# Taking GpSimd's remaining arithmetic out of a five-stage fp32 kernel and giving it to VectorE

## The chip, the cores and the metric

The program runs on one NeuronCore of a Trainium2 chip. A core has five engines that run their own instruction streams: TensorE (PE in the profile; PEld is its weight load), VectorE (DVE), ScalarE (ACT), GpSimd (POOL) and SyncE (SP), and 16 DMA engines. The metric is the device time of one execution in microseconds; lower is better.

## The reference

Everything is float32 on 1024 tokens of width 1024. The first block is an FFN, a token mixer and a second FFN, each with a norm ahead and a norm behind; the second block prepends 16 tokens and applies an even layer (a linear recurrence, RG-LRU, beside a chunked state-space scan, SSD) and an odd layer (stick-breaking attention).

```python
def swiglu(x, w_gate, w_up, w_down):
    return (jax.nn.silu(x @ w_gate) * (x @ w_up)) @ w_down

def partial_rope(t, pos):          # the first 16 of 64 dimensions of a head
    ...
    out = jnp.concatenate([x1 * cos - x2 * sin, x2 * cos + x1 * sin, rest], axis=-1)

def first_block(x, ...):
    f1 = swiglu(rms_norm(x, ffn1_pre_g[l]), ffn1_w_gate[l], ffn1_w_up[l], ffn1_w_down[l])
    x = x + FFN_RESIDUAL_WEIGHT * rms_norm(f1, ffn1_post_g[l])
    m = token_mixer(rms_norm(x, mix_pre_g[l]), w_in[l], ...)
    x = x + rms_norm(m, mix_post_g[l])
    f2 = swiglu(rms_norm(x, ffn2_pre_g[l]), ...)
    x = x + FFN_RESIDUAL_WEIGHT * rms_norm(f2, ffn2_post_g[l])

# SSD of the even layer, in chunks
y_diag = jnp.einsum('bcgls,bgecls,bcsgep->bclgep', cb, decay, X)
y_off = jnp.einsum('bclgn,bcgepn,bgecl->bclgep', Cc, states, jnp.exp(a_cum))
y = (y_diag + y_off).reshape(bsz, L + pad, SSD_HEADS, SSD_HEAD_DIM)
y = y + xh * ssd_d[:, None]
```

## The kernel before

The stages follow one another: first FFN (0 to about 692 us), mixer (from about 705), second FFN (about 1350 to 2035), even layer (about 2050 to 2850), odd layer (to the end). A float32 product is made of three TensorE products: an operand is split into a high part (ScalarE, a rounded copy) and a low part (VectorE, the difference). So a split is one ScalarE and one VectorE instruction, and TensorE waits for the second.

**The order of instructions.** Each piece of work is a Python generator that yields the engine it wants ("P" TensorE, "A" ScalarE, "V" VectorE, "G" GpSimd, "D" DMA) and a planned cost. A planner (`Sched`) picks among the ready requests by priority and planned time, and so writes one fixed order for each engine. On the chip each engine runs its order strictly, and a late instruction holds all behind it. The planner's costs of a VectorE and a GpSimd instruction don't depend on each other.

**FFN.** Both big products use seven block products in place of eight. The differences of token blocks that these need are made in `tokens` (`diff`, lines 796 to 818): the high parts are subtracted on VectorE (L802), the low parts on GpSimd (L804), the two are added (L806), T2 adds two more, and the result is split again (ScalarE, then L815 on VectorE). Tiles named `T` are these. The splits of gate and up weights are L473 (`wl`), those of the down operands L1049 (`dl`), the sums of down's results into `acc` L1104 (`pdn` is PSUM, `sg` SBUF). GpSimd makes the inner sums of h (L956) and of the down weights (L1006), which both versions keep.

Down's last pass (`ci` = 2) finishes rows of 128 tokens one after the other, and `post` (from L1185) then normalises each: sum of squares (ScalarE), the reciprocal root (tiny VectorE instructions L306 to L310), gain and residual. Six of eight rows have the gain multiplied by GpSimd in `scale` (L1220) and then one fused VectorE instruction (L1209); the other two have two VectorE instructions (L1212, L1215). Behind a row come the norm of the next stage (L603), the transposes by TensorE (L554) and the split of the transposed activations (L542), for which the next stage's first product waits.

**Mixer.** A rotary head is copied to `rx`, shuffled into `ry` (L1821), multiplied on VectorE (L1823) and GpSimd (L1825), added on VectorE (L1827), and split; the low half of queries (L1406) and keys (L1427) is GpSimd's.

**Even layer.** Per chunk GpSimd scales X by the decay (L2720). `ssd_back` makes `x*d + psy` in four VectorE instructions (L2780, `psy` is PSUM), then `ea*pso` (L2784), and four GpSimd instructions add `ea` (L2789). `gated` (L2972) multiplies on GpSimd.

Of the kernel before, what the change touches and what calls it, by code (L numbers as in the profile page):

```python
# [18 lines left out]
P = 128  # L19
# [637 lines left out]
def ffn_stage(c, A, first, rows0, wg, wu, wd, gpost, res, rows, nxt, meta=None, cols=None):  # L657
# [12 lines left out]
    with ExitStack() as ctx:  # L670
# [120 lines left out]
        def tokens():  # L791
# [4 lines left out]
            def diff(hi, lo, a, b_, extra, ev):  # L796
# [6 lines left out]
                yield ("G", pool_tt(512))  # L803
                nc.gpsimd.tensor_sub(u, a[1].bitcast(F32), b_[1].bitcast(F32))  # L804
# [284 lines left out]
        def evac_d(ci, p, t, ps):  # L1089
# [95 lines left out]
        def post(t, done):  # L1185
# [4 lines left out]
            scaled = Ev()  # L1190
            on_pool = t not in (5, 7)
            if on_pool:
                sch.spawn(scale(t, scaled), 1, tt)
# [11 lines left out]
            if on_pool:  # L1205
                yield scaled
                yield ev_x[t]
                yield ("V", dve(1024))
                nc.vector.scalar_tensor_tensor(acc[t], acc[t], r, xs[t], op0=ALU.mult, op1=ALU.add)  # L1209
            else:  # L1210
                yield ("V", dve(1024))
                nc.vector.scalar_tensor_tensor(acc[t], acc[t], r, gp[0], op0=ALU.mult, op1=ALU.mult)  # L1212
                yield ev_x[t]
                yield ("V", dve(1024))
                nc.vector.tensor_add(acc[t], acc[t], xs[t])  # L1215
            yield from rows.put(t, acc[t], junk)

        def scale(t, ev):
            t_ = yield ("G", pool_tt(1024))
            nc.gpsimd.tensor_mul(acc[t], acc[t], gp[0])  # L1220
            ev.set(t_)
# [76 lines left out]
        ahead = Stream(c, "G", shared=True)  # L1298
# [36 lines left out]
class Attention:  # L1335
# [58 lines left out]
    def evac_q(self, u, h, src, scale, ps):  # L1394
# [3 lines left out]
        for e in range(2):  # L1398
# [4 lines left out]
            on_pool = ps is None  # L1403
            t = yield ("G", pool_tt(512)) if on_pool else ("V", dve(512))
            if scale == 1.0:
                (nc.gpsimd if on_pool else nc.vector).tensor_sub(q[R2[e], 2 + e], s, hi)  # L1406
# [9 lines left out]
    def evac_k(self, u, tok, src, ps, ev):  # L1416
# [4 lines left out]
        for e in range(2):  # L1421
# [3 lines left out]
            on_pool = ps is None  # L1425
            t = yield ("G", pool_tt(n)) if on_pool else ("V", dve(n))
            (nc.gpsimd if on_pool else nc.vector).tensor_sub(ks[e][o, tok], s, ks[e][R2[e], tok].bitcast(F32))  # L1427
# [197 lines left out]
    def out_proj(self, oD, w_out, after, ready, evac, last=KD - 1):  # L1625
# [10 lines left out]
        def load():  # L1636
            yield after
            WO.extend(c.new_A())
            yield from W.into(w_out, 0, WO[0], WO[1], ev_w, 2, "V" if self.col0 else "GV")
# [77 lines left out]
def mixer_stage(c, A, rows0, prm, w_in, forget_b, lams, subln, rope, w_out, gpost, res, rows):  # L1717
# [3 lines left out]
    with ExitStack() as ctx:  # L1721
# [89 lines left out]
        def rope_evac(u, w, h, ps):  # L1811
# [265 lines left out]
        def out_rows(t, ps, tag):  # L2077
# [24 lines left out]
            eng = "GV"[t // 4]  # L2102
            yield (eng, pool_tt(1024) if eng == "G" else dve(1024))
            (nc.gpsimd if eng == "G" else nc.vector).tensor_add(y, y, x)
            T.r_x.release(sch.free[eng])
# [337 lines left out]
def even_stage(c, A, rows0, prm, w_in, lru_wa, lru_wx, dt_bias, a_log, ssd_d, w_out, meta, res, rows):  # L2443
# [212 lines left out]
    def ssd_front(g):  # L2656
# [7 lines left out]
        for i, (t0, T) in enumerate(CHUNKS):  # L2664
# [54 lines left out]
            yield ("G", pool_tt(512))  # L2719
            nc.gpsimd.tensor_tensor(xe[:T], xd[:T], dec[:T].unsqueeze(2).to_broadcast([T, 8, 64]), op=ALU.mult)  # L2720
# [12 lines left out]
    def ssd_back(g):  # L2733

        St = None
        for i, (t0, T) in enumerate(CHUNKS):
# [44 lines left out]
            ss.release(t)  # L2781
            if i > 0:
                t = yield ("V", dve(512))
# [462 lines left out]
```

## Time and profile before

| what | value |
| --- | --- |
| three runs | 3673.99, 3675.97 (median), 3686.52 us |
| the profiled execution, its own time | 3678.58 us |
| its span (first to last instruction) | 3676.9 us |
| TensorE busy in the span | 94% |
| VectorE, ScalarE, GpSimd busy | 75%, 46%, 17% |
| mean granted TensorE clock | 0.978 of full |

The busy shares are means over stages of different kinds. The sums of the prediction are made against 3678.58 us, the profiled execution's own time, which lies 2.61 us above the median.

### The profile page before, as it was taken

The numbers are of one execution on the slowest core, as the hardware profiler recorded it, in microseconds if no ns is written. First come the engines' busy times: TensorE is split into PE (matmuls) and PEld (weight loads), VectorE is DVE, ScalarE is ACT, GpSimd is POOL, SyncE is SP. The second block draws the span as 40 slices with busy tenths as digits, with TensorE's granted clock in tenths as the row PEclk, the third lists the DMA queues.
The fourth block names the chain that finished last, engine by engine and source line by source line (L and its number), as shares of the span: only waits on it lengthen the run. The fifth ranks groups of instructions, "written<-read, shape, count | busy, mean of one in ns | idle before, by whom it ended". The sixth has DMA issues, their size and how long they took to land. (4 is left out here: it accounts for less than half of the span.)

```text
span 3676.9 us, 51971 instructions
## 1 busy us (share of the span) xinstructions
PE 3469.4 (94%) x19675; PEld 2950.4 (80%) x19675; DVE 2756.6 (75%) x4900; ACT 1694.3 (46%) x3449; POOL 641.5 (17%) x577
## 2 busy tenths in 40 slices
PE   8899999799999899999999899998999999999989
PEld 7688888578878777888887899988878888888867
DVE  7876699977888769766799768568623788878784
ACT  4333244455656643333344437446412565656561
POOL 3211145411110114211354112113100000000000
PEclk9999999899999999999999999999999999999999
DMA  4232372311210342332561334234332111110123
GB/s 147 87 108 100 120 264 69 128 53 43 68 51 28 104 154 82 106 109 89 183 215 52 111 70 79 68 84 87 119 116 92 55 35 30 30 35 26 35 82 104
DMA packets 296627, 332.52 MB, mean 90 GB/s; under 512 B 17620, under 2 KB 220544, under 8 KB 296376
## 3 DMA queue, kind: packets, MB, share of 16 engines
q1 hardware_dynamic: 290584, 308.15, 27.6%
q10 hardware_dynamic: 5792, 21.04, 1.5%
q8 instruction: 155, 2.54, 0.3%
q14 instruction: 96, 0.79, 0.1%
HBM read 250.80 MB, written 78.35 MB: 90 GB/s over the span
## 5 line engine op out<-in xcount | busy, mean ns | idle before, releaser
L336 PE MATMUL pe<-Ah,wh 128*128 128x260 f32 (+1 forms) x1184 | 344.1, 291 | 21.6 <-ACT sz L224 7.5
L338 PE MATMUL pe<-Ah,wl 128*128 128x260 f32 (+1 forms) x1184 | 339.3, 287 | 0.0
L337 PE MATMUL pe<-Al,wh 128*128 128x260 f32 (+1 forms) x1184 | 339.0, 287 | 0.0
L224 ACT CAST wh<-w 128x512 fp32r<-128x512 f32 x280 | 162.5, 619 | 271.1 <-PE pst L337 193.0
L892 DVE TENSOR_TENSOR sg<-sg,pst 128x512 f32<-128x512 f32 x280 | 186.5, 682 | 114.6 <-PE pst L338 114.3
L337 PE MATMUL pst<-Al,wh 128*128 128x512 f32 x640 | 253.4, 396 | 2.2 <-DVE Al L815 2.2
L473 DVE TENSOR_TENSOR wl<-w,wh 128x512 fp32r<-128x512 f32 x280 | 209.9, 772 | 58.9 <-ACT wh L224 57.5
L336 PE MATMUL pst<-Ah,wh 128*128 128x512 f32 x640 | 251.8, 393 | 0.0
L338 PE MATMUL pst<-Ah,wl 128*128 128x512 f32 x640 | 251.6, 393 | 0.0
L337 PE MATMUL pdn<-dl,dh 128*128 128x512 f32 x592 | 233.4, 394 | 16.3 <-DVE dl L1049 16.3
L336 PEld LDWEIGHTS pe<-Ah,wh 128*128 128x128 f32 (+1 forms) x1184 | 225.8, 191 | 26.0 <-ACT sz L224 8.0
L1511 DVE TENSOR_TENSOR tl<-ptr,th 128x512 fp32r<-128x512 f32 (+2 forms) x344 | 198.0, 592 | 63.6 <-ACT th L224 61.2
L224 ACT CAST th<-ptr 128x512 fp32r<-128x512 f32 (+2 forms) x344 | 170.7, 515 | 133.4 <-PE ptr L1560 128.2
L338 PE MATMUL pdn<-dh,dl 128*128 128x512 f32 x592 | 231.7, 391 | 0.0
L336 PE MATMUL pdn<-dh 128*128 128x512 f32 x592 | 231.6, 391 | 0.0
L956 POOL TENSOR_TENSOR h<-h 128x512 f32<-128x512 f32 x88 | 134.5, 1529 | 535.6 <-DVE h L938 530.5
L337 PEld LDWEIGHTS pe<-Al,wh 128*128 128x128 f32 (+1 forms) x1184 | 225.7, 191 | 1.5 <-issue 0.5
L338 PEld LDWEIGHTS pe<-Ah,wl 128*128 128x128 f32 (+1 forms) x1184 | 225.5, 191 | 0.8
L2219 DVE TENSOR_TENSOR_SCAN kt<-kt,onec 128x392 f32<-128x392 f32 (+6 forms) x224 | 202.5, 914 | 26.1 <-ACT kt L224 25.0
L224 ACT CAST wh<-wr 128x1024 fp32r<-128x1024 f32 (+2 forms) x116 | 119.0, 1026 | 212.0 <-PE pwo L3045 121.7
L473 DVE TENSOR_TENSOR wl<-wr,wh 128x1024 fp32r<-128x1024 f32 (+1 forms) x110 | 138.8, 1263 | 86.0 <-ACT wh L224 85.7
L336 PE MATMUL pst<-T,wh 128*128 128x512 f32 x480 | 188.4, 395 | 10.9 <-ACT T L224 10.8
(555 smaller groups left out, 10496.0 us busy)
## 6 DMA issues: line engine op xcount, KB each, us to landing
hD<-h SPq DMA_DIRECT2D x22, 1792.0 KB
w<-in_ffn_w_gate_dram SPq DMA_DIRECT2D x20, 1024.0 KB
w<-in_ffn_w_up_dram SPq DMA_DIRECT2D x20, 1024.0 KB
d<-hD SPq DMA_DIRECT2D x18, 1024.0 KB
wr<-in_even_w_in_dram SPq DMA_DIRECT2D x36, 512.0 KB
wr<-in_odd_w_in_dram SPq DMA_DIRECT2D x32, 512.0 KB
wr<-in_w_in_dram SPq DMA_DIRECT2D x24, 512.0 KB
d<-in_ffn_w_down_dram SPq DMA_DIRECT2D x8, 1024.0 KB
```

What stands on the lines that cost most here:

```text
L224: self.last = _o(*a, **k)
L336: nc.tensor.matmul(ps, wh, xh, start=start, stop=False)
L337: nc.tensor.matmul(ps, wh, xl, start=False, stop=False)
L338: nc.tensor.matmul(ps, wl, xh, start=False, stop=stop)
L473: (nc.gpsimd if eng == "G" else nc.vector).tensor_sub(lo, raw, hi.bitcast(F32))
L892: nc.vector.tensor_add(dst, src, ps)
L956: nc.gpsimd.tensor_sub(q[:, o], q[:, a], q[:, b_])
L1511: nc.vector.tensor_sub(tl[:rows, :n], ptr[:rows, :n], th[:rows, :n].bitcast(F32))
L2219: nc.vector.tensor_tensor_scan(rev, rev, c.one.to_broadcast([P, m]), kt[:, k0 + m:k0 + m + 1], op0=ALU.mult, op1=ALU.mult)
```

## The change

All but the inner sums (L956, L1006), the adds into `acc` of the first two passes of down (L1104, `ci` = 1) and memsets leaves GpSimd for VectorE: the low differences of `tokens` (L804, 32 instructions), 16 adds into `acc` in down's last pass, the gain of `post` (12; all rows now take the two-instruction form, at L1202 and L1205 of the changed kernel), the splits of the next stage's first weights and of some output weights (L473, 12), the rope products (16) and low halves (32), four residual adds behind the mixer, the decay product (18) and the gates (16). In `ssd_back`, `psy` is added into `ea` in one VectorE instruction and the four fused instructions then read `ea`, so that GpSimd's 64 adds are gone with 16 VectorE instructions in their place. TensorE's instructions are the same in number.

```diff
@@ diff(): T1 to T4
-                yield ("G", pool_tt(512))
-                nc.gpsimd.tensor_sub(u, a[1].bitcast(F32), b_[1].bitcast(F32))
+                yield ("V", dve(512))
+                nc.vector.tensor_sub(u, a[1].bitcast(F32), b_[1].bitcast(F32))
...
@@ sums into acc
+                eng = "V" if ci == 2 else "G"
...
-                    yield from add(c01, c01, "G", v)
+                    yield from add(c01, c01, eng, v)
...
-                    eng = "V" if ci == 2 else "G"
                     yield from add(c10, c10, eng, v)
-                    tt = yield from add(c11, c11, "G", v)
+                    tt = yield from add(c11, c11, eng, v)
...
@@ post()
-            on_pool = t not in (5, 7)
-            if on_pool:
-                sch.spawn(scale(t, scaled), 1, tt)
...
-            if on_pool:
-                yield scaled
-                yield ev_x[t]
-                yield ("V", dve(1024))
-                nc.vector.scalar_tensor_tensor(acc[t], acc[t], r, xs[t], op0=ALU.mult, op1=ALU.add)
-            else:
...
+            yield ("V", dve(1024))
+            nc.vector.scalar_tensor_tensor(acc[t], acc[t], r, gp[0], op0=ALU.mult, op1=ALU.mult)
+            yield ev_x[t]
+            yield ("V", dve(1024))
+            nc.vector.tensor_add(acc[t], acc[t], xs[t])
...
-        def scale(t, ev):
-            t_ = yield ("G", pool_tt(1024))
-            nc.gpsimd.tensor_mul(acc[t], acc[t], gp[0])
...
-        ahead = Stream(c, "G", shared=True)
+        ahead = Stream(c, "V", shared=True)
...
@@ rope_evac(); evac_q, evac_k, the decay product and gated change engine in the same way
-            t = yield ("G", pool_tt(512))
-            nc.gpsimd.tensor_mul(y, y, rp[:, 1])
             yield ("V", dve(512))
+            nc.vector.tensor_mul(y, y, rp[:, 1])
+            t = yield ("V", dve(512))
             nc.vector.tensor_add(x, x, y)
...
@@ ssd_back()
+            y = psy
+            if i > 0:
+                t = yield ("V", dve(512))
+                nc.vector.tensor_mul(ea, ea, pso[:, :, :T])
+                ss.release(t)
+                t = yield ("V", dve(512))
+                nc.vector.tensor_add(ea, ea, psy)
+                ss.release(t)
+                y = ea
...
-                nc.vector.scalar_tensor_tensor(x, x, dcol[:, u:u + 1], psy[:, q, :T], op0=ALU.mult, op1=ALU.add)
...
-                t = yield ("G", 4 * pool_tt(P))
-                for q in range(4):
-                    x = XC[4 * g + q][1][:, tk]
-                    nc.gpsimd.tensor_add(x, x, ea[:, q])
-                r_ea.release(t)
+                nc.vector.scalar_tensor_tensor(x, x, dcol[:, u:u + 1], y[:, q, :T], op0=ALU.mult, op1=ALU.add)
+            (r_ea if i > 0 else ss).release(t)
```

The planner decides again with every engine that is changed, so the order moves too. First place: VectorE in the first FFN while T4 is being made. Before:

```order
L806 TENSOR_TENSOR sg<-sg 128x512
L761 TENSOR_TENSOR w<-w 128x4x128
L802 TENSOR_TENSOR sg<-Ah,T_509 128x512
L815 TENSOR_TENSOR T_650<-sg,T_647 128x512
L761 TENSOR_TENSOR w<-w 128x4x128
L806 TENSOR_TENSOR sg<-sg 128x512
L802 TENSOR_TENSOR sg<-Ah,T_509 128x512
L473 TENSOR_TENSOR wl<-w,wh 128x512
L815 TENSOR_TENSOR T_925<-sg,T_924 128x512
L473 TENSOR_TENSOR wl<-w,wh 128x512
L892 TENSOR_TENSOR sg<-sg,pst 128x512 x2
```

In the changed kernel, where the same differences are made:

```order
L806 TENSOR_TENSOR sg<-sg 128x512
L802 TENSOR_TENSOR sg<-Ah,T_509 128x512
L804 TENSOR_TENSOR sg<-Al,T_510 128x512
L815 TENSOR_TENSOR T_648<-sg,T_644 128x512
L806 TENSOR_TENSOR sg<-sg 128x512
L802 TENSOR_TENSOR sg<-Ah,T_509 128x512
L804 TENSOR_TENSOR sg<-Al,T_510 128x512
L815 TENSOR_TENSOR T_801<-sg,T_800 128x512
L806 TENSOR_TENSOR sg<-sg 128x512
```

The low difference L804 now stands on VectorE beside its high one, and the weight splits (L473) and preparations (L761) that stood between the steps have gone to other places in the order. Second place: VectorE at the end of the first FFN's down product, where the first rows are normalised (`rs_` are the reciprocal roots). Before:

```order
L306 TENSOR_SCALAR rs_v<-ssp 128x2
L1049 TENSOR_TENSOR sg<-d,sg 128x512
L1049 TENSOR_TENSOR dl<-d,dh 128x512
L306 TENSOR_SCALAR rs_v<-ssp 128x2
L308 SCALAR_TENSOR_TENSOR rs_a<-rs_y 128x2
L309 TENSOR_TENSOR rs_a<-rs_a,rs_v 128x2
L310 SCALAR_TENSOR_TENSOR rs_y<-rs_a,rs_y 128x2
L1209 SCALAR_TENSOR_TENSOR acc<-acc,rs_y,gp 128x1024
L1049 TENSOR_TENSOR dl<-d,dh 128x512
L308 SCALAR_TENSOR_TENSOR rs_a<-rs_y 128x2
L1209 SCALAR_TENSOR_TENSOR acc<-acc,rs_y,gp 128x1024
```

In the changed kernel, the end of the same piece:

```order
L310 SCALAR_TENSOR_TENSOR rs_y<-rs_a,rs_y 128x2
L308 SCALAR_TENSOR_TENSOR rs_a<-rs_y 128x2
L1104 TENSOR_TENSOR acc<-acc,pdn 128x512
L309 TENSOR_TENSOR rs_a<-rs_a,rs_v 128x2
L1202 SCALAR_TENSOR_TENSOR acc<-acc,rs_y,gp 128x1024
L310 SCALAR_TENSOR_TENSOR rs_y<-rs_a,rs_y 128x2
L1202 SCALAR_TENSOR_TENSOR acc<-acc,rs_y,gp 128x1024
L1205 TENSOR_TENSOR acc<-acc,gp 128x1024 x2
L1202 SCALAR_TENSOR_TENSOR acc<-acc,rs_y,gp 128x1024 x2
L1205 TENSOR_TENSOR acc<-acc,d 128x1024 x2
```

Each row that had one fused instruction (L1209) now has two (L1202, L1205); the tiny L306 to L310 stay where the chain needs them.

## Rows read from the trace of the kernel before

**Rows 1.** The page, busy time of each engine over the span.

```profile
PE 3469.4 (94%) x19675; PEld 2950.4 (80%) x19675; DVE 2756.6 (75%) x4900; ACT 1694.3 (46%) x3449; POOL 641.5 (17%) x577
```

**Rows 2.** Groups of POOL by form: busy us, mean ns, then the idle time ahead.

```profile
L2789 POOL TENSOR_TENSOR xc<-xc,ea 128x128 f32<-128x128 f32 x64 | 42.7, 698 | 120.7 <-DVE ea L2784 120.7
L804 POOL TENSOR_TENSOR sg<-Al 128x512 f32<-128x512 f32 x16 | 37.9, 2384 | 133.3 <-DVE Al L542 109.2 <-DVE sg L806 18.5 <-DVE h L938 5.5
L804 POOL TENSOR_TENSOR sg<-T,Al 128x512 f32<-128x512 f32 x8 | 12.6, 1589 | 26.8 <-DVE sg L806 13.3 <-DVE T L815 8.5 <-DVE h L938 5.1
L1220 POOL TENSOR_TENSOR acc<-acc,gp 128x1024 f32<-128x1024 f32 x12 | 31.1, 2611 | 21.8 <-ACT junk L224 21.8
```

**Rows 3.** The same view for DVE.

```profile
L1049 DVE TENSOR_TENSOR dl<-d,dh 128x512 fp32r<-128x512 f32 x170 | 172.0, 1022 | 4.7 <-ACT dh L224 4.1
L1104 DVE TENSOR_TENSOR acc<-acc,pdn 128x512 f32<-128x512 f32 x152 | 95.5, 676 | 0.1
L1209 DVE SCALAR_TENSOR_TENSOR acc<-acc,rs_y,d 128x1024 f32<-128x1024 f32 x8 | 10.1, 1279 | 0.1
```

**Rows 4.** Timeline of DVE and POOL: start us, us, operation.

```profile
486.67 2.73 POOL L1006 TENSOR_TENSOR d<-d 128x1024 f32<-128x1024 f32 x1 [1.90 <-DVE dl L1049]
487.06 2.47 DVE L1104 TENSOR_TENSOR acc<-acc,pdn 128x512 f32<-128x512 f32 x4
699.59 2.39 POOL L1220 TENSOR_TENSOR acc<-acc,gp 128x1024 f32<-128x1024 f32 x1 [3.30 <-ACT junk L224]
699.67 2.32 DVE L308 SCALAR_TENSOR_TENSOR rs_a<-rs_y 128x2 f32<-128x2 f32 x1
```

**Rows 5.** Busy us by stage: PE, PEld, DVE, ACT, POOL, then PE clock.

```profile
40.00:140.00 100.00, 87.55 (x379) 68.98 (x379) 88.89 (x127) 33.71 (x60) 43.68 (x23) 0.97 0.12 40
460.00:644.00 184.00, 183.26 (x807) 151.02 (x806) 173.41 (x210) 87.37 (x155) 92.54 (x44) 1.00 0.47 166
660.00:680.00 20.00, 13.59 (x51) 10.39 (x51) 19.82 (x21) 8.26 (x18) 13.55 (x5) 0.85 0.42 133
680.00:705.00 25.00, 19.40 (x83) 15.70 (x81) 24.90 (x42) 14.43 (x30) 7.43 (x4) 0.78 0.43 148
1380.00:1480.00 100.00, 92.46 (x389) 72.55 (x390) 92.00 (x133) 36.88 (x64) 40.87 (x22) 0.97 0.22 71
2200.00:2600.00 400.00, 372.14 (x3012) 356.09 (x3012) 297.72 (x513) 225.16 (x367) 87.22 (x106) 0.96 0.38 80
```

**Rows 6.** Timeline, the differences T1 to T4: idle before, releaser in brackets.

```profile
81.60 1.76 DVE L806 TENSOR_TENSOR sg<-sg 128x512 f32<-128x512 f32 x1 [5.19 <-POOL sg L804]
106.70 0.80 PE L336 MATMUL pst<-T,wh 128*128 128x512 f32 x1 [5.09 <-ACT T L224]
```

**Rows 7.** Timeline, end of the first FFN and start of the mixer.

```profile
664.60 10.79 POOL L1220 TENSOR_TENSOR acc<-acc,gp 128x1024 f32<-128x1024 f32 x4 [5.42 <-ACT junk L224]
665.66 4.70 DVE L1049 TENSOR_TENSOR dl<-d,dh 128x512 fp32r<-128x512 f32 x2
675.99 0.79 PE L337 MATMUL pdn<-dl,dh 128*128 128x512 f32 x1 [5.37 <-DVE dl L1049]
705.08 0.50 PE L336 MATMUL pd<-Ah,wh 128*128 128x512 f32 x1 [0.35 <-DVE Al L542]
```

**Rows 8.** Timeline, the same place in the second FFN.

```profile
2019.18 0.80 PE L337 MATMUL pdn<-dl,dh 128*128 128x512 f32 x1 [5.36 <-DVE dl L1049]
```

**Rows 9.** Timeline, first rotary head of the mixer.

```profile
726.09 2.53 POOL L1825 TENSOR_TENSOR ry<-ry,rope 128x512 f32<-128x512 f32 x2
727.42 1.75 DVE L1827 TENSOR_TENSOR rx<-rx,ry 128x512 f32<-128x512 f32 x1 [3.98 <-POOL ry L1825]
732.03 3.42 DVE L603 TENSOR_SCALAR pt<-pt,rs_y 128x1024 f32<-128x1024 f32 x2
733.83 0.48 PE L554 MATMUL ptf<-ident,pt 128*128 128x128 f32 x1 [3.01 <-DVE pt L603]
767.52 0.63 PE L1500 MATMUL psc<-ks('d', 0)0_5394,qs 128*128 128x320 f32 x1 [3.58 <-POOL ks('d', 0)0_5394 L1427]
```

More of the change, by code (lines that the diff above doesn't have):

```diff
@@ L1189, in post @@
             nc.scalar.activation(junk(), acc[t], AF.Square, accum_out=ss[g][:, t - g:t - g + 1])
-            scaled = Ev()
-            on_pool = t not in (5, 7)
-            if on_pool:
-                sch.spawn(scale(t, scaled), 1, tt)
             left[g] = left.get(g, len(rows.members(t))) - 1
@@ L1204, in post @@
             r = rs[g][:, t - g:t - g + 1]
-            if on_pool:
-                yield scaled
-                yield ev_x[t]
-                yield ("V", dve(1024))
-                nc.vector.scalar_tensor_tensor(acc[t], acc[t], r, xs[t], op0=ALU.mult, op1=ALU.add)
-            else:
[L1211 to L1215, printed above, removed]
+            yield ("V", dve(1024))
[3 more added lines that the diff above has]
+            nc.vector.tensor_add(acc[t], acc[t], xs[t])
             yield from rows.put(t, acc[t], junk)
-        def scale(t, ev):
-            t_ = yield ("G", pool_tt(1024))
-            nc.gpsimd.tensor_mul(acc[t], acc[t], gp[0])
-            ev.set(t_)
         def residual():
@@ L1402, in evac_q @@
             hi = q[R2[e], e].bitcast(F32)
-            on_pool = ps is None
-            t = yield ("G", pool_tt(512)) if on_pool else ("V", dve(512))
+            t = yield ("V", dve(512))
             if scale == 1.0:
-                (nc.gpsimd if on_pool else nc.vector).tensor_sub(q[R2[e], 2 + e], s, hi)
+                nc.vector.tensor_sub(q[R2[e], 2 + e], s, hi)
             else:
@@ L1424, in evac_k @@
             nc.scalar.copy(ks[e][R2[e], tok], s)
-            on_pool = ps is None
-            t = yield ("G", pool_tt(n)) if on_pool else ("V", dve(n))
-            (nc.gpsimd if on_pool else nc.vector).tensor_sub(ks[e][o, tok], s, ks[e][R2[e], tok].bitcast(F32))
+            t = yield ("V", dve(n))
+            nc.vector.tensor_sub(ks[e][o, tok], s, ks[e][R2[e], tok].bitcast(F32))
         if ps is not None:
@@ L1638, in load @@
             WO.extend(c.new_A())
-            yield from W.into(w_out, 0, WO[0], WO[1], ev_w, 2, "V" if self.col0 else "GV")
+            yield from W.into(w_out, 0, WO[0], WO[1], ev_w, 2, "V")
             for t in range(8):
@@ L2101, in out_rows @@
             nc.vector.scalar_tensor_tensor(y, y, rs[g][:, t - g:t - g + 1], gps[0], op0=ALU.mult, op1=ALU.mult)
[L2102 to L2105, printed above, removed]
+            tt = yield ("V", dve(1024))
+            nc.vector.tensor_add(y, y, x)
+            T.r_x.release(tt)
             yield from rows.put(t, y, junk)
@@ L2718, in ssd_front @@
             act_t(m, m, AF.Exp)
-            yield ("G", pool_tt(512))
-            nc.gpsimd.tensor_tensor(xe[:T], xd[:T], dec[:T].unsqueeze(2).to_broadcast([T, 8, 64]), op=ALU.mult)
+            yield ("V", dve(512))
+            nc.vector.tensor_tensor(xe[:T], xd[:T], dec[:T].unsqueeze(2).to_broadcast([T, 8, 64]), op=ALU.mult)
             if i > 0:
@@ L2775, in ssd_back @@
             r_cb.release(t)
+            y = psy
[3 more added lines that the diff above has]
+                ss.release(t)
+                t = yield ("V", dve(512))
+                nc.vector.tensor_add(ea, ea, psy)
+                ss.release(t)
+                y = ea
             t = yield ("V", 4 * dve(T))
@@ L2779, in ssd_back @@
                 x = XC[u][1][:, tk]
-                nc.vector.scalar_tensor_tensor(x, x, dcol[:, u:u + 1], psy[:, q, :T], op0=ALU.mult, op1=ALU.add)
-            ss.release(t)
-            if i > 0:
-                t = yield ("V", dve(512))
-                nc.vector.tensor_mul(ea, ea, pso[:, :, :T])
-                ss.release(t)
-                t = yield ("G", 4 * pool_tt(P))
-                for q in range(4):
-                    x = XC[4 * g + q][1][:, tk]
-                    nc.gpsimd.tensor_add(x, x, ea[:, q])
-                r_ea.release(t)
+                nc.vector.scalar_tensor_tensor(x, x, dcol[:, u:u + 1], y[:, q, :T], op0=ALU.mult, op1=ALU.add)
+            (r_ea if i > 0 else ss).release(t)
         for u in (8 + g, 10 + g):
@@ L2970, in gated @@
         for j in range(2):
-            t = yield ("G", pool_tt(LH))
-            nc.gpsimd.tensor_mul(ig[:, j], ig[:, j], CV[2 * b + j][1][:, hi])
+            t = yield ("V", dve(LH))
+            nc.vector.tensor_mul(ig[:, j], ig[:, j], CV[2 * b + j][1][:, hi])
             if h == 1:
@@ L3144, in even_stage @@
     W2 = Stream(c, pool=pj, nraw=2, shared=False)
-    sch.spawn(W2.into(w_out, D, WO[0], WO[1], ev_wl, 2, "VVG"), 2)
+    sch.spawn(W2.into(w_out, D, WO[0], WO[1], ev_wl, 2, "V"), 2)
     sch.spawn(loads(), 2)
```

## The prediction

> **What bounds the kernel now.** I read the page first: TensorE is busy 94% of the span, VectorE 75%, GpSimd 17% [rows 1]. So the time is TensorE's work plus the places where TensorE waits, some 207 us in all (3676.9 − 3469.4), and an edit on the other engines pays only through those places. The table by stage then shows where they lie: in the first FFN's difference part TensorE is idle 12.5 of 100 us, at the end of its down product 6.4 of 20, in the next 25 us another 5.6, in the second FFN's difference part 7.5 of 100, in the middle of the even layer 27.9 of 400; in the body of the down product only 0.7 of 184 [rows 5]. In all but the even layer VectorE is 89 to nearly 100% busy there. The timelines say what TensorE waits for: splits that VectorE delivers late, and a GpSimd result [rows 6 to 9].
>
> A busy VectorE is not always working. Its clean price for 512 elements is 0.62 us a piece (four in 2.47 us), and one of the inputs there is PSUM; GpSimd's 2.73 us instruction ran beside all four and cost them nothing [rows 4]. But a two-column instruction that started 0.08 us after a GpSimd multiplication took 2.32 us and ended when that one did [rows 4], and while GpSimd ran four multiplications in a row, two splits of 512, with both inputs in SBUF, took 4.70 us instead of 1.24 [rows 7]. The means say the same over the kernel: the split with two SBUF inputs 1.02 us, the sum with a PSUM input 0.68 [rows 3]. So a GpSimd instruction holds up VectorE for its own length, when VectorE wants two things from SBUF. The Trainium skill, "SBUF — State Buffer", section "Who interferes with whom", states this: VectorE's second read port is GpSimd's only one, whoever starts first keeps it for a whole instruction, and a VectorE instruction with at most one SBUF input outside the two-port modes isn't touched. The trace agrees, with 2.32 beside 2.39 us on the one side and 2.47 us for four on the other.
>
> **The change part by part.** *What VectorE takes on.* 512-wide: 32 low differences, 16 adds, 16 rope products and 32 low halves, 18 decay products, 16 gates, 16 adds of `psy`: 146 × 0.62 = 91 us. 1024-wide: 12 adds in `post`, four residual adds, ten splits (two small ones left out), at 1.28 us as for L1209 [rows 3]: 33 us. Together 124 us, on an engine that is busy 2757. *What it gets back* is the time in which it was held. In the stretch just read it was held 4.70 − 1.24 = 3.46 us of two GpSimd instructions of 2.70, a share of 0.64. At that share a 512-wide GpSimd instruction of 1.59 us [rows 2] costs VectorE 1.02 and doing it itself 0.62; a 1024-wide one of 2.61 costs 1.67, against 1.28. Break-even lies at a share of about 0.4 to 0.5. So I expect VectorE's busy time to move little, and look at the chains in which GpSimd's result or a held instruction was what TensorE waited for.
>
> *First FFN, differences.* 16 of the 32 low differences are here; those that read Al alone take 2.38 us on GpSimd [rows 2]. VectorE stood still 5.19 us for one, and TensorE then waits 5.09 us for the T that hangs on such a chain [rows 6]. VectorE pays 16 × 0.62 = 9.9 us. It gets back the 5.19, and 0.64 of 16 GpSimd instructions, eight of 2.38 and eight of 1.59 us [rows 2]: 0.64 × 31.8 = 20.3. That is 15.6 us net, more than the 12.5 that TensorE is idle, so TensorE's idle time is the cap. I take the 5.09 whole and half of the rest: −9. From 0 (the weight splits that the new order moves behind the differences, see the order, become late instead) to −12.5.
>
> *Second FFN, differences.* The same instructions, 7.5 us idle: 9/12.5 of it, −5.5; from 0 to −7.5.
>
> *End of the first FFN, to the mixer's first product at 705.08.* GpSimd's 13.55 us of 660 to 680 and 7.43 of 680 to 705 [rows 5] are nearly all moved. VectorE gets back 0.64 × 21.0 = 13.4 us and pays, up to the last row needed, four of the six added sums and the two splits: 6 × 1.28 = 7.7. That is 5.7 net. The 5.37 us that TensorE waits for a split at 675.99 [rows 7] is that queue. The split stood behind held instructions. Shorter waits also spare clock: TensorE was granted 0.85 and 0.78 in the two stretches [rows 5], and its product right after the wait took 0.79 us [rows 7]; at full clock its 13.59 + 19.40 busy us would be 6.3 shorter at most, of which I count a fifth. −7; from −3 (the two-instruction form lies in front of what the transposes need, and half the gain goes there) to −12 (all idle time of both stretches).
>
> *End of the second FFN.* The same code and the same wait, 5.36 us [rows 8]: −7, from −3 to −12.
>
> *Start of the mixer.* Line L1827 waits 3.98 us for the GpSimd product and is then held itself, 1.75 us for 0.62; two norms take 3.42 us where I allow 2 × 1.28 at most [rows 9]. That is 3.98 + 1.13 + 0.86 = 6.0 back, against two products and four low halves (6 × 0.62 = 3.7). TensorE's waits of 3.01 and 3.58 us [rows 9] hang on these; the second goes straight, since the keys' low half no longer queues on GpSimd. Between the net 2.3 and the 6.6 of the two waits I take −4; if nothing is returned it is +3.7.
>
> *Even layer, other mixer heads, outputs.* Here no wait of TensorE is put down to GpSimd. In 2200 to 2600 GpSimd is busy 87.2 us and VectorE 74% [rows 5], so a held instruction delays work that mostly has slack. 64 adds of 0.70 us [rows 2] go for 16 of 0.62; decay, gates and these together are 50 × 0.62 = 31 us for VectorE, against 87.2 × 0.64 = 56 if it was held as at the FFN's end and 30 at a share of 0.34. I take 0, from +15 (half of the 31 on the path, nothing back) to −14 (half of the idle 27.9). The fused instructions lose their PSUM input in the bargain, but no GpSimd arithmetic is left in this layer to hold them. In the body of the down product, where TensorE has no idle time to give back, 8 adds per FFN come to VectorE (5 us), and it has 184 − 173.4 = 10.6 spare [rows 5]: 0. The odd layer's GpSimd work is memsets: 0.
>
> Sum: −9 − 5.5 − 7 − 7 − 4 + 0 = −32.5. From the profiled execution's 3678.58 that is 3646, from the median, 2.6 lower, 3643. All weak ends together: +12.7 (3689); all strong ends: −64.5 (3611).
>
> **The rivals.** *Nothing gained (3665 to 3687).* VectorE stays as full as it was in the FFN ends, does 124 us more, and the waits come back under another name: TensorE waits for weight splits that now queue behind differences and gain instructions. For it: 19.82 and 24.90 busy of 20 and 25 us [rows 5], so every instruction taken on delays all behind it. Against it: a good part of that busy time is holding, 3.46 of 4.70 us where it can be read. Chance 0.13.
>
> *Slower, by 12 to 25 us (3688 to 3700).* VectorE becomes the bound in the even layer and the mixer's heads, because there its instructions mostly read PSUM, were never held, and so get nothing back: then the 31 us of the even layer and the head's 48 × 0.62 = 30 us are pure addition, and at about a third of the sum on TensorE's path (+20), with half of the FFN's gain lost to the same cause, the change loses. It decides where the held share falls below the break-even of 0.4. For it: the PSUM sums that weren't touched [rows 4]. Against it: VectorE has a quarter of the even layer free [rows 5]. The Trainium skill's page "Perfetto Trace Analysis", section "Optimizing Scalar/DVE Operations", leans this way for a saturated VectorE: moving work off it, to GpSimd even, may pay, though it warns that the two share a port. Chance 0.11.
>
> *More than forecast (3611 to 3626).* The held time returns in the even layer and in every head too, since the fixed order passes each delay on: strong ends everywhere, −50 to −64. For it: 27.9 us idle in those 400 us alone. Against it: no wait there names GpSimd. Chance 0.15.
>
> **How the numbers follow.** The forecast itself (−15 to −50, 3626 to 3661) has 0.61. About 0.3%, 11 us, is what a measurement of this kernel can tell from no change. Faster by more: 0.61 + 0.15 = 0.76; within: 0.13; slower: 0.11. The range for 8 in 10 leaves out half of the slower case, the upper half of the nothing case and the far end of the strong one: 3614 to 3672.
>
> **What would show it.** Right: GpSimd's busy time falls to the inner sums, adds and memsets; L1049's mean falls from 1.02 to about 0.8 us (its L1006 neighbours stay), L308 never takes 2.3 us; VectorE's busy total changes by less than 40 us; TensorE's 5.09, 5.37 and 5.36 us waits are gone or under 2; the mixer's first product comes near 689 (both FFN terms together). Wrong: VectorE's total rises by 80 us or more, new waits of TensorE for `wl` (L473) or `Al` (L542) of like size stand in the same stretches, or the even layer's 2200 to 2600 piece gets longer.

## The result and the profile after

The changed kernel takes 3621.84 us (four runs, 3619.37 to 3625.5), the kernel before 3676.26 (3673.99 to 3686.52): a ratio of 0.9847, interval 0.9826 to 0.9869, or about 54 us less. The profiled execution took 3619.37 us, 59.2 below the profiled one of before. The forecast was 3643, from 3614 to 3672. The time lies inside that range, but not where the likeliest case put it (3626 to 3661): it fell into the rival "more than forecast" (3611 to 3626), which had 0.15.

The page of the changed kernel, busy time of each engine; [rows 1] answers to it:

```profile
PE 3441.5 (95%) x19675; PEld 2934.7 (81%) x19675; DVE 2764.0 (76%) x5074; ACT 1699.2 (47%) x3451; POOL 324.0 (9%) x355
```

GpSimd lost 317.5 us of work. VectorE took on 124 us by the forecast's count, and its total rose by 7.4. If that count is right, 117 us of what had counted as VectorE's work was time in which it was held. TensorE performs the same 19,675 matmuls in 27.9 us less busy time, at a mean granted clock of 0.985 in place of 0.978. So nearly half of the 59.3 us by which the span is shorter is busy time of TensorE, and the rest is idle time.

The table by stage of the changed kernel (columns and stretches as in [rows 5]; the later stretches hold somewhat later work now):

```profile
40.00:140.00 100.00, 87.11 (x387) 70.92 (x386) 97.08 (x148) 35.09 (x61) 13.03 (x8) 0.93 0.17 58
460.00:644.00 184.00, 182.85 (x805) 150.67 (x804) 175.11 (x215) 88.33 (x157) 87.15 (x40) 1.00 0.48 166
660.00:680.00 20.00, 20.00 (x90) 16.57 (x89) 19.71 (x34) 12.81 (x27) 0.00 (x0) 1.00 0.65 215
680.00:705.00 25.00, 17.23 (x77) 13.97 (x76) 24.80 (x48) 14.71 (x32) 0.00 (x0) 0.86 0.31 106
1380.00:1480.00 100.00, 94.85 (x407) 75.83 (x405) 92.55 (x139) 33.71 (x60) 17.46 (x12) 0.98 0.26 84
2200.00:2600.00 400.00, 377.62 (x3074) 359.42 (x3073) 287.82 (x531) 216.17 (x352) 4.56 (x14) 0.97 0.38 87
```

At the end of the down product (660 to 680) TensorE was busy 13.59 of 20 us and is now busy throughout, at full clock in place of 0.85; VectorE is as full as before but performs 34 instructions where it performed 21. In the difference part (40 to 140) TensorE gained nothing: it is busy 87.11 us in place of 87.55.

Two groups of VectorE in the changed kernel, the first as in [rows 3]; the second is the tiny instruction of [rows 4]:

```profile
L1049 DVE TENSOR_TENSOR dl<-d,dh 128x512 fp32r<-128x512 f32 x170 | 157.7, 940 | 5.2 <-ACT dh L224 4.8
...
L308 DVE SCALAR_TENSOR_TENSOR rs_a<-rs_y 128x2 f32<-128x2 f32 x16 | 2.5, 155 | 1.1 <-ACT rs_y L224 1.0
```

The down splits are held still (g_all below shows by what); L308 is never held: its longest takes 0.16 us. TensorE's waits in the changed kernel's timeline, as in [rows 6, 7]:

```profile
106.64 0.79 PE L338 MATMUL pst<-Ah,wl 128*128 128x512 f32 x1 [12.89 <-DVE wl L473]
...
683.93 3.54 PE L554 MATMUL ptf<-ident,gp 128*128 128x128 f32 x16 [3.20 <-DVE gp L603]
...
694.03 0.79 PE L336 MATMUL pd<-Ah,wh 128*128 128x512 f32 x1 [3.53 <-DVE Al L542]
```

The 5.37 us wait for a down split is gone, and the mixer's first product starts at 694.03 in place of 705.08. But the waits for L603 and L542 in front of it have grown. The first of these lines is of the kernel before, where the wait for L542 was 0.35 us; the others are of the changed kernel at the end of the second FFN:

```profile
693.38 0.33 PE L554 MATMUL ptf<-ident,gp 128*128 128x128 f32 x1 [1.25 <-DVE gp L603]
...
1994.70 3.51 PE L554 MATMUL ptf<-ident,gp 128*128 128x128 f32 x16 [3.20 <-DVE gp L603]
...
2005.46 0.59 PE L336 MATMUL pe<-Ah,wh 128*128 128x260 f32 x1 [4.19 <-DVE Al L542]
```

In the difference part one wait of 12.89 us, for a weight split, stands where several smaller ones stood.

**Where it went, by stage.** The table below is read from the timelines of all profiled executions: the time between the first matmul of one stage and of the next (first `pdn`, first `pd`, first transpose of the second FFN's tokens, its first `pdn`, first `pe`, first product of the even layer's output). Kernels with the same code in a stage agree there within about 2 us (first column: 469.3 to 471.5), in the even layer within 5 (584.9 to 589.7).

| kernel | FFN 1, gate/up | FFN 1, down and end | mixer | FFN 2, gate/up | FFN 2, down and end | even layer |
| --- | --- | --- | --- | --- | --- | --- |
| before | 471.0 | 234.1 | 646.5 | 462.2 | 235.8 | 597.9 |
| changed | 469.3 | 224.7 | 627.8 | 458.4 | 225.2 | 584.9 |
| x_order | 466.0 | 226.2 | 620.5 | 458.4 | 228.9 | 589.4 |
| y_order | 472.4 | 228.1 | 649.3 | 462.3 | 228.1 | 598.5 |
| h_read | 471.3 | 230.7 | 628.6 | 458.3 | 231.7 | 588.9 |
| h_write | 470.3 | 224.7 | 626.7 | 459.0 | 225.4 | 586.4 |
| f_prio | 465.6 | 225.1 | 625.9 | 458.8 | 227.3 | 585.6 |
| g_all | 471.2 | 223.6 | 625.8 | 459.9 | 223.6 | 586.0 |
| nofuse | 470.4 | 224.6 | 628.0 | 459.0 | 225.0 | 586.3 |
| u_xegat | 471.5 | 224.5 | 627.2 | 459.0 | 225.2 | 598.7 |
| u_tok | 472.2 | 224.5 | 628.4 | 462.2 | 226.9 | 586.3 |
| u_rope | 469.4 | 224.3 | 644.9 | 458.4 | 225.2 | 589.7 |
| c1 | 465.0 | 226.2 | 619.2 | 457.6 | 228.6 | 585.2 |
| c2 | 463.4 | 224.3 | 619.8 | 458.6 | 225.9 | 586.0 |

What is left behind the even layer took 1029.4 us before, 1027.3 in the changed kernel and up to 1032.2 in the others, so no gain is shown there.

Three of these stages in the columns of [rows 5], each before and then changed: gate/up of the first FFN, its down product and end, and the even layer, of which the last line is u_xegat (below).

```profile
0.00:471.00 471.00, 446.47 (x1939) 362.39 (x1940) 340.73 (x553) 154.56 (x265) 100.76 (x69) 0.99 0.34 110
0.00:469.31 469.31, 442.76 (x1940) 361.56 (x1941) 346.77 (x569) 155.37 (x264) 68.26 (x52) 0.99 0.33 110
...
471.00:705.08 234.08, 220.88 (x958) 180.75 (x956) 224.10 (x279) 115.91 (x213) 112.80 (x54) 0.96 0.45 157
469.31:694.03 224.72, 215.81 (x957) 177.98 (x955) 215.99 (x300) 117.70 (x217) 80.39 (x37) 0.99 0.48 164
...
2049.62:2647.48 597.86, 563.37 (x4576) 541.42 (x4576) 426.56 (x734) 306.82 (x512) 98.95 (x136) 0.96 0.36 81
2005.46:2590.33 584.87, 556.43 (x4577) 535.72 (x4577) 429.77 (x781) 308.80 (x512) 7.67 (x38) 0.97 0.36 82
2007.46:2606.13 598.67, 559.83 (x4576) 538.38 (x4577) 432.41 (x747) 305.49 (x509) 57.03 (x72) 0.97 0.36 80
```

VectorE gains most in the down product: it performs 21 instructions more there and is busy 8.1 us less. In gate/up it is busy 6.0 us more with 16 instructions more. In the even layer it is busy 3.2 us more, where the forecast counted 31. Of the 13.0 us by which that layer is shorter, 6.1 are idle time of TensorE and 6.9 busy time, with the same matmuls.

### The profile page after: what moved, and what is told of

Read it like the earlier page. It is cut to its first block, busy times and chain, and to the rows that moved or that the text cites. A ratio compares the mean times of both kernels' runs of the same rounds, so it can differ in the third digit from the quotient of the medians.

```text
span 3617.6 us, 51732 instructions
## 1 busy us (share of the span) xinstructions
PE 3441.5 (95%) x19675; PEld 2934.7 (81%) x19675; DVE 2764.0 (76%) x5074; ACT 1699.2 (47%) x3451; POOL 324.0 (9%) x355
## 4 chain that ended last, share of the span: by engine, by line
PE 70%; DVE 19%; ACT 5%; issue 3%; DMA 2%; SPq 1%; POOL 0%; ACTq 0%; DVEq 0%; POOLq 0%
PE pst L338 7%; PE pst L337 7%; PE pst L336 7%; PE po L1526 3%; PE pe L336 3%; PE pe L338 3%; PE pe L337 3%; DVE kt L2201 3%; PE pdn L337 2%; PE ptr L1543 2%; PE pdn L338 2%; PE pdn L336 2%; DVE dl L1049 2%; PE pwo L1662 2%; PE pwo L1663 2%
## 5 line engine op out<-in xcount | busy, mean ns | idle before, releaser
L338 PE MATMUL pst<-Ah,wl 128*128 128x512 f32 x640 | 252.0, 394 | 12.9 <-DVE wl L473 12.9
L473 DVE TENSOR_TENSOR wl<-w,wh 128x512 fp32r<-128x512 f32 x280 | 212.1, 783 | 56.9 <-ACT wh L224 55.4
L956 POOL TENSOR_TENSOR h<-h 128x512 f32<-128x512 f32 x88 | 132.8, 1509 | 1354.6 <-DVE h L938 1349.4
L473 DVE TENSOR_TENSOR wl<-wr,wh 128x1024 fp32r<-128x1024 f32 (+2 forms) x116 | 137.6, 1186 | 76.4 <-ACT wh L224 76.1
```

The lines of the kernel that those rows point to most:

```text
L338: nc.tensor.matmul(ps, wl, xh, start=False, stop=stop)
L473: (nc.gpsimd if eng == "G" else nc.vector).tensor_sub(lo, raw, hi.bitcast(F32))
L956: nc.gpsimd.tensor_sub(q[:, o], q[:, a], q[:, b_])
```

## The experiments

The theory: the gain is the time in which GpSimd's instructions, reading SBUF, keep VectorE out. Its rivals: the planner's new order did it; a GpSimd result was merely late in a chain; any GpSimd work beside VectorE costs it.

**The order or the engine: x_order and y_order.** x_order is the kernel before with every moved request still planned as GpSimd's, and the instruction issued on VectorE. y_order is the changed kernel with its order, and low differences, the adds of `post` (which the kernel before had inside a VectorE instruction), rope products, low halves, decay and gates are issued on GpSimd.

```diff
@@ x_order, against the kernel before
                 yield ("G", pool_tt(512))
-                nc.gpsimd.tensor_sub(u, a[1].bitcast(F32), b_[1].bitcast(F32))
+                nc.vector.tensor_sub(u, a[1].bitcast(F32), b_[1].bitcast(F32))
@@ y_order, against the changed kernel
                 yield ("V", dve(512))
-                nc.vector.tensor_sub(u, a[1].bitcast(F32), b_[1].bitcast(F32))
+                nc.gpsimd.tensor_sub(u, a[1].bitcast(F32), b_[1].bitcast(F32))
```

> The kernel before, its order planned as before (the moved instructions are planned as GpSimd's), but each of them is issued on VectorE; forms as before (12 gain products of 1024, 64 small adds of 128). Theory of holding (VectorE loses the time in which a GpSimd instruction keeps it out): most of the 54 us comes, 3622 to 3642, since nothing holds VectorE although the order is the old one. Rival, the new order did it: near 3676, at least 3660.

> The changed kernel, order planned as changed, but low differences, the 16 adds of post (L1205), rope products and low halves, decay and gates are executed by GpSimd. Theory of holding: the gain goes, 3665 to 3710 (each of these holds VectorE again, and the order is not made for its length). Rival, the new order did it: at most 3635.

From here on the kernel before had medians of 3680.7 to 3681.3 us in place of 3676.26, so ratios compare best, or runs of one session. x_order took 3622.6 us (ratio 0.9844, 0.983 to 0.9859), as fast as the changed kernel and at the good end of what holding was to give. y_order took 3670.36 (0.9974, 0.9964 to 0.9984), in its range too: with 227 us of GpSimd work again, only 11 us are left of the gain. So the engine does it. The order only shifts the gain between stages: the old one wins more in the mixer (26.0 against 18.7 us) and perhaps less in the even layer (8.5 against 13.0, at the edge of the scatter). The pages, x_order first, then y_order:

```profile
PE 3453.3 (95%) x19675; PEld 2943.8 (81%) x19675; DVE 2757.9 (76%) x5122; ACT 1693.7 (47%) x3449; POOL 325.1 (9%) x355
```

```profile
PE 3460.2 (94%) x19675; PEld 2948.6 (80%) x19675; DVE 2758.0 (75%) x4944; ACT 1699.4 (46%) x3451; POOL 551.9 (15%) x485
```

VectorE's total is the same in both, though the second has 227 us more GpSimd work beside it and 178 fewer instructions of VectorE's own.

**Holding, with no result to wait for: h_read and h_write.** Both are the changed kernel with its order, and extra GpSimd work in `post` whose result nobody reads, started by the sum of squares.

```diff
+            if t not in (5, 7):
+                nc.gpsimd.tensor_copy(dm[0][:, :1], ss[g][:, t - g:t - g + 1])
+                for _ in range(3):                 # h_write: nine memsets of dm[0]
+                    nc.gpsimd.tensor_mul(dm[0], gp[0][:, :240], gp[0][:, 240:480])
```

> The changed kernel with the same order on the other engines, plus GpSimd work whose result nobody reads: behind the sum of squares of each of 12 rows (six per FFN), three products of 128x240 from SBUF. Theory of holding: 36 instructions of about 0.9 us hold VectorE for 0.64 of 32 us; half of that on TensorE's path: +6 to +14 us, all at the two ends of the FFNs. Rival, it was only the length of a GpSimd result that the chain waited for: 0, since nobody waits for these.

> The control of the run with products nobody reads: nine memsets of 128x240 in place of the three products, about as long together. Theory of holding by reads of SBUF: within 3 us of the changed kernel, VectorE's instructions at their clean length. Rival, any GpSimd work beside VectorE costs it: as much as the products.

h_read took 3639.24 us (3636.2 to 3639.81), 17 more than the changed kernel and than h_write (3621.6) beside it. That is above the 6 to 14 expected. By the table h_read loses 6.0 and 6.5 us at the two FFN ends; the even layer's 4 is within what that stage scatters. VectorE is busy 12.8 us more than in the changed kernel. h_read in its page and in the timeline (VectorE and GpSimd, just ahead of the first normalised row, then TensorE's wait for that row):

```profile
PE 3451.0 (95%) x19675; PEld 2941.3 (81%) x19675; DVE 2776.8 (76%) x5074; ACT 1699.7 (47%) x3451; POOL 370.3 (10%) x403
...
663.48 3.44 POOL L1196 TENSOR_TENSOR dm<-gp 128x240 f32<-128x240 f32 x3
664.03 1.20 DVE L1049 TENSOR_TENSOR op<-d,op 128x512 fp32r<-128x512 f32 x1
665.16 1.19 DVE L1049 TENSOR_TENSOR dl<-d,dh 128x512 fp32r<-128x512 f32 x1
666.27 1.19 DVE L1049 TENSOR_TENSOR op<-d,op 128x512 fp32r<-128x512 f32 x1
...
690.27 3.70 PE L554 MATMUL ptf<-ident,gp 128*128 128x128 f32 x16 [7.82 <-DVE gp L603]
```

The same place in h_write:

```profile
662.69 3.18 POOL L1196 MEMSET dm<- 128x240 f32 x9
662.70 0.68 DVE L1049 TENSOR_TENSOR dl<-d,dh 128x512 fp32r<-128x512 f32 x1
663.30 0.68 DVE L1049 TENSOR_TENSOR op<-d,op 128x512 fp32r<-128x512 f32 x1
663.91 0.69 DVE L1049 TENSOR_TENSOR dl<-d,dh 128x512 fp32r<-128x512 f32 x1
```

The splits step by 1.1 us beside GpSimd's reads, one for each of its instructions, and by 0.6 beside its memsets. TensorE's wait for the row's norm grew from 3.20 to 7.82 us with h_read and is 3.20 with h_write. No instruction reads the results. The views put one wait of TensorE at each FFN end down to the extra work, but of like size in both runs (1.32 us in h_read, 1.22 and 1.04 in h_write), and the changed kernel waits 1.04 and 1.07 us in the same places. So the rival of the late result can't explain the loss, and the rival of any work at all is out.

**The difference part: f_prio and u_tok.** f_prio gives the differences other than T2 a lower priority than the weight splits; u_tok gives the low differences back to GpSimd.

```diff
@@ f_prio
-                    ..., event("Tk", name, k)), 1, sch.time)
+                    ..., event("Tk", name, k)), 1 if name == "T2" else 3, sch.time)
@@ u_tok
-                yield ("V", dve(512))
-                nc.vector.tensor_sub(u, ...)
+                yield ("G", pool_tt(512))
+                nc.gpsimd.tensor_sub(u, ...)
```

> The changed kernel, but the planner takes the differences T1, T3 and T4 behind the weight splits (priority 3 in place of 1; T2, wanted first, stays). The changed kernel's TensorE waits 12.89 us at 93.7 us for a weight split (wl), with 22 us of difference work in a row on VectorE ahead of it. If that order is what ate the first FFN's forecast 9 us: the 12.89 us wait falls under 5, the first FFN's products start 5 to 9 us earlier, the time is 3609 to 3617. Rival, VectorE is simply full there (97 of 100 us busy) and another wait takes its place: within 3 us of 3622.

> The changed kernel, but the 32 low differences of the FFNs (L804) are GpSimd's again, planned so. The first FFN's differences gave 1.7 us and the second's 3.3 in place of 9 and 5.5. If the move itself was worth little there: TensorE's progress at 150 us within 3 us of the changed kernel, the whole +2 to +6. If it was worth the forecast and the new order hid it: +8 or more at 150 us.

f_prio: 3620.45 us, no difference from the changed kernel in the whole. But its first stage is 3.7 us shorter, and the 12.89 us wait is gone. In its place, f_prio's timeline and table by stage show:

```profile
105.08 0.80 PE L337 MATMUL pst<-T,wh 128*128 128x512 f32 x1 [3.43 <-DVE T L815]
```

```profile
40.00:140.00 100.00, 93.86 (x406) 74.19 (x405) 95.96 (x149) 35.31 (x61) 13.13 (x8) 0.97 0.14 47
77.00:130.00 53.00, 46.85 (x186) 35.70 (x185) 51.61 (x87) 20.54 (x36) 0.00 (x0) 0.94 0.22 75
```

GpSimd's 13.13 us are inner sums before and behind the second stretch, in which it does nothing at all. VectorE, busy 51.61 of 53 us there, is held by nobody and full all the same, and TensorE is idle 6.15. So VectorE's own work is most likely the bound here, and the order decides how much TensorE loses. u_tok (3630.63, one run) is 9 us above the changed kernel, more than expected; by the table 2.9 us of that are in the first FFN's gate/up, near the scatter (469.3 to 471.5 with the same code), and 3.8 in the second's.

**The mixer: u_rope.** Rope products and low halves back on GpSimd.

```diff
-            yield ("V", dve(512))
-            nc.vector.tensor_mul(y, y, rp[:, 1])
+            t = yield ("G", pool_tt(512))
+            nc.gpsimd.tensor_mul(y, y, rp[:, 1])
```

> The changed kernel, but rope products and the low halves of rotary heads (16 and 32 instructions) are GpSimd's again, planned so. The mixer gave 16 us where 4 were forecast for its start and 0 for the rest. Theory of holding: 71 us of GpSimd come back, 12 to 18 of the 16 us are lost, in steps at each of the eight rotary heads. Rival, the mixer's gain came from its output splits and residual sums: at most +4.

3643.65 us (one run); 17.1 of the mixer's 18.7 us are lost, by the table, as the theory expected. The wait of [rows 9] is back, in u_rope's timeline:

```profile
756.91 0.64 PE L1485 MATMUL psc<-ks('d', 0)0_5394,qs 128*128 128x320 f32 x1 [3.58 <-POOL ks('d', 0)0_5394 L1412]
```

**The even layer: u_xegat and nofuse.** u_xegat has decay and gates on GpSimd; nofuse has the scan's old form with its 64 small adds on VectorE.

```diff
@@ u_xegat
-            yield ("V", dve(512))
-            nc.vector.tensor_tensor(xe[:T], ...)
+            yield ("G", pool_tt(512))
+            nc.gpsimd.tensor_tensor(xe[:T], ...)
@@ nofuse
+                t = yield ("V", 4 * dve(P))
+                for q in range(4):
+                    nc.vector.tensor_add(x, x, ea[:, q])
```

> The changed kernel, but the even layer's decay products (18) and gates (16) are GpSimd's again, planned so. Theory of holding: 34 x 1.4 = 48 us of GpSimd hold VectorE, half of the even layer's 16 us comes back: +5 to +10 us. Rival, the even layer's gain came from the scan's 64 adds alone: within 3 us of 3622.

> The changed kernel, but the even layer's scan keeps the old form on VectorE: four fused instructions from psy, then 64 adds of 128 on VectorE in place of 16 of 512. Even layer of the changed kernel: 16 us shorter. If the fused form matters: 48 more instructions, 64 x 0.28 against 16 x 0.62 = +8 us of VectorE, of which 2 to 8 us come to the end. Rival, only the engine matters: within 2 us of 3622 on the even layer.

u_xegat: 3638.43 us (one run), and its even layer, 598.7 us, is as long as that of before: the 34 decay and gate products alone cost all 13 us, more than expected. nofuse: 3624.82 (one run), even layer 586.3; the fused form is worth 1.4 us there, inside the scatter, so that is left undecided. In the even layer, VectorE's groups by form, of the changed kernel, then of u_xegat, then L2696's counterpart in the kernel before:

```profile
L2479 DVE SCALAR_TENSOR_TENSOR cv<-xb,prm,cv 128x1040 f32<-128x1040 f32 x24 | 31.0, 1293 | 0.3
L2696 DVE TENSOR_SCALAR ab<-ab,dT 128x128 f32<-128x128 f32 x128 | 28.1, 280 | 0.4
```

```profile
L2696 DVE TENSOR_SCALAR ab<-ab,dT 128x128 f32<-128x128 f32 x128 | 36.3, 351 | 0.5
...
L2479 DVE SCALAR_TENSOR_TENSOR cv<-xb,prm,cv 128x1040 f32<-128x1040 f32 x24 | 34.2, 1423 | 0.8
```

```profile
L2714 DVE TENSOR_SCALAR ab<-ab,dT 128x128 f32<-128x128 f32 x128 | 37.8, 363 | 0.5
```

TensorE's groups then show who pays, before, changed, and in u_xegat:

```profile
L2750 PE MATMUL psy<-ab,xd 128*64 128x128 f32 (+1 forms) x288 | 20.7, 280 | 5.4 <-DVE ab L2725 5.4
...
L2732 PE MATMUL psy<-ab,xd 128*64 128x128 f32 (+1 forms) x288 | 19.3, 276 | 3.2 <-DVE ab L2707 3.2
...
L2732 PE MATMUL psy<-ab,xd 128*64 128x128 f32 (+1 forms) x288 | 20.5, 279 | 11.5 <-DVE ab L2707 11.5
```

The held L2696 scales `ab`, the matrices go through ScalarE to L2707, and TensorE waits 11.5 us for that. No line of this chain names GpSimd. The same wait was 5.4 us before, so the two kernels lose the 13 us in part at different places; what they share is the held instruction.

**The rest of GpSimd's arithmetic: g_all.** The inner sums L956 and L1006 and the remaining adds move too.

```diff
-                eng = "V" if ci == 2 else "G"
+                eng = "V"
-                    yield ("G", pool_tt(512))
-                    nc.gpsimd.tensor_sub(q[:, o], q[:, a], q[:, b_])
+                    yield ("V", dve(512))
+                    nc.vector.tensor_sub(q[:, o], q[:, a], q[:, b_])
```

> The changed kernel with GpSimd's remaining arithmetic moved too: 88 inner sums of h, 48 inner sums of the down weights, 24 adds into acc: VectorE takes on 112 x 0.62 + 8 x 0.62 + 40 x 1.22 = 123 us. Theory of holding: it gets back at least as much (its total rises by less than 20 us, the down splits fall to 0.62 to 0.70 us each), and the time stays within 8 us of 3622, since TensorE has no idle time in those stretches to win. Rival, VectorE is the bound in the down product (95% busy): its total rises by 60 us or more and the time by 20 to 40 us.

3619.29 us (0.9835, 0.9819 to 0.9852), as the changed kernel within its scatter, as the theory expected. Its page, the down splits and the body of the down product:

```profile
PE 3445.3 (95%) x19675; PEld 2937.3 (81%) x19675; DVE 2765.7 (76%) x5234; ACT 1699.8 (47%) x3451; POOL 32.0 (1%) x195
```

```profile
L1049 DVE TENSOR_TENSOR dl<-d,dh 128x512 fp32r<-128x512 f32 x170 | 114.6, 689 | 10.4 <-ACT dh L224 10.4
```

```profile
460.00:644.00 184.00, 184.00 (x813) 152.24 (x812) 167.67 (x257) 89.87 (x159) 0.00 (x0) 1.00 0.46 167
```

VectorE takes on 123 us and its total rises by 1.7. In the down product it is busy 167.67 us with 257 instructions, against 175.11 with 215: there, doing GpSimd's work itself costs it less than being held by it; over the kernel it costs the same.

**Put together: c1 and c2.** c1 has x_order's FFNs and mixer and the changed even layer; c2 also moves what g_all moves.

```diff
@@ c1, in the FFN (likewise in the mixer)
                 yield ("G", pool_tt(512))
-                nc.gpsimd.tensor_sub(u, a[1].bitcast(F32), b_[1].bitcast(F32))
+                nc.vector.tensor_sub(u, a[1].bitcast(F32), b_[1].bitcast(F32))
@@ c1, in the even layer, as in the changed kernel
-                    nc.gpsimd.tensor_add(x, x, ea[:, q])
+                nc.vector.tensor_add(ea, ea, psy)
```

> A mixture: FFNs and mixer in the old planned order and forms with the moved instructions on VectorE (as in the run of the old order), even layer as in the changed kernel. By TensorE's progress the old order reached the even layer's start 50 us ahead of before, the changed kernel 43; the changed even layer is worth 16, the other 9. If the stages are independent: 66 us below before, 3612 to 3617, 5 to 10 below the changed kernel. Rival, later stages absorb it: within 3 us of 3622.

> The same mixture with GpSimd's inner sums and adds on VectorE too, so that it has no arithmetic of 512 or 1024 left. Theory of holding with the break-even found (123 us moved raised VectorE's total by 2): within 4 us of the mixture, 3608 to 3618. Rival, a VectorE without GpSimd's help is too full in the old order: 10 us or more above the mixture.

c1: 3614.93 us (3613.86 to 3615.72; ratio 0.9823, 0.981 to 0.9837), in its range and below every run of the changed kernel, though the intervals of the two ratios overlap. c2: 3611.46 (3606.43 to 3623.7; 0.9816, 0.9796 to 0.9836), no clear gain over c1. Both beat the kernel before, and c1 most likely the changed one, by some 7 us. c1's stages are within 1.3 us of those of the kernels that they were taken from, so the stages are nearly independent.

## Why the prediction was right, and where its steps were off

The direction and the mechanism held: GpSimd's arithmetic holds VectorE, and giving it away pays although VectorE takes on 124 us. Its terms against the table:

| term | forecast | measured |
| --- | --- | --- |
| first FFN, differences | −9 | −1.7 (other kernels with this code: −1.6 to +0.5) |
| second FFN, differences | −5.5 | −3.8 |
| end of the first FFN | −7 | −9.4 |
| end of the second FFN | −7 | −10.6 |
| start of the mixer | −4 | −5.8 of the mixer's −18.7 |
| other mixer heads, even layer, outputs | 0 | −12.9 (heads), −13.0 (even), −2.1 (outputs and odd layer) |
| sum | −32.5 | −59.3 |

That the number came inside the range is in part luck: 9 us too much for the differences cancel a third of the 28 too little for what was put at 0.

The start of the mixer is taken from its first `pd` to the second head's first `pq`: 130.2 us before, 124.4 after.

*The share of 0.64* holds about where it was read and not elsewhere. In the first FFN's down product and end GpSimd lost 32.4 us and VectorE's busy time fell by 8.1, although it took on at least 12.7 by the forecast's prices (eight adds, six adds in `post`): a share of 0.64 or more. In gate/up it got back 3.9 of 32.5 us, a share of 0.12; in the even layer 28 of 91, 0.30. Over the kernel it was 117 of 317.5, 0.37, and in g_all 121 of 292, 0.41. That is at or under the break-even that the prediction named, and the change pays all the same: VectorE's total doesn't move, as forecast, and what counts is where the held instruction stood. h_read fits: VectorE's total rises by 12.8 us, and the FFN ends lose 12.5.

*The differences.* The term failed in its sum and in its choice from the range. The sum had VectorE 15.6 us better off; over gate/up of the first FFN its busy time rose by 6.0, so that of the 9.9 us that it took on it got back 3.9 and not 25.5. The term named the case (the weight splits become late) as the weak end and took more than the middle. In the changed kernel VectorE makes differences from one weight split at 77.62 us to the next at 105.91, with five other instructions between, and a wait of 12.89 us for that split is what came. f_prio shows that the order was about half of it: 3.7 of the 7.3 us missed. The other half is most likely that VectorE is full there with work of its own.

*The ends of the FFNs.* Mechanism right, size a third short: no wait there is for a down split any more. The reserve for clock was too small: 660 to 680 went from 0.85 to full. The waits of 3.20 and 3.53 us for L603 and L542, longer than before, are what is left there, and the first product behind the second still takes 0.79 us.

*Other heads and even layer, 0.* This is the step that failed, by 26 us without the outputs, whose 2.1 are within scatter. Its reason was that no wait of TensorE there is put down to GpSimd and that VectorE is 74% busy, so that a delay has slack. But a held instruction is booked as busy and as VectorE's, and what it delays is booked to the engine in between; u_xegat has 13 us of loss without one such line. And the sum looked for waits alone: of the even layer's 13.0 us only 6.1 are TensorE's idle time, and 6.9 are busy time with the same matmuls, at a granted clock of 0.97 in place of 0.96. Over the kernel that is 27.9 us, where the sum had a fifth of 6.3 us at each FFN end for it. No run separates the clock from the waits: they moved together. The rival "more than forecast" had the first of these reasons. It was given 0.15 for want of a wait that names GpSimd, which is no evidence against it.

The rival "nothing gained" is out except in the difference part, where it is what happened. "Slower" is out: the even layer's VectorE did get its time back, all but 3.2 of the 31 us.

Of what was to show it: GpSimd's fall, L308 and VectorE's total (+7.4) came as said. L1049's mean fell to 0.94 and not to 0.8. The 5.37 us wait went, the 5.09 became 12.89. The mixer began at 694 and not 689, by the missing difference term. Two of its signs of being wrong came too: a wait for `wl` of 12.89 us in the difference part, and waits for `Al` of 3.53 and 4.19 us at the FFN ends. The first ate the term of the differences; at the FFN ends the waits that went were longer than those that came.

What stays open: why the order planned for before is some 7 us better in the mixer, what the fused form of the scan is worth, and how much of TensorE's shorter busy time follows from the shorter waits.

## What to carry to other kernels

A second elementwise engine can cost the first one as much time as it saves it. Compare the mean of one kind of instruction with both inputs in SBUF and with one in PSUM. If they differ (1.02 and 0.68 us here), charge each reading helper instruction to the first engine too, and ask stage by stage how much of it is held: here VectorE's total was the same within 10 us with 641, 324 and 32 us of GpSimd work beside it, while the time fell by 54 us at the first step and by nothing clear at the second. Look for such losses in busy time and in instruction means, since the chain of waits need not name them. And read the order of the changed engine for long rows of one kind: what stands behind 28 us of them is the next wait.

## What the runs showed of the hardware

- A memset on GpSimd doesn't hold VectorE, a product does: 108 memsets (33.4 us) cost nothing, 36 products (39.4 us) cost 17. The Trainium skill, "SBUF — State Buffer", section "Who interferes with whom", says so of GpSimd instructions that only write; the trace agrees, with VectorE's steps of 0.6 and 1.1 us.
- It is not only instructions with two full inputs from SBUF: L2696, a TENSOR_SCALAR with one, took 351 ns with 57 us of GpSimd work in its layer and 280 with 8.
- Under steady reads the two engines take turns: one VectorE split per GpSimd instruction of 1.1 us, in the stretch shown of h_read.
- After the 12.89 us wait of the changed kernel TensorE's products took 0.63 us each until 110.2 us and 0.39 from 110.7 on: first mostly the lower of its two clock levels (1.2 and 2.4 GHz), then the upper. Its windows, in the columns of [rows 5]:

```profile
106.60:112.00 5.40, 5.36 (x16) 4.29 (x17) 5.40 (x10) 4.16 (x9) 0.00 (x0) 0.66 0.09 18
112.00:117.00 5.00, 5.00 (x24) 4.12 (x23) 4.79 (x8) 0.77 (x2) 0.00 (x0) 1.00 1.05 345
```
